# A mixture-of-experts layer on one core: seven of eight row blocks of the experts' weights in two parts, where it was six, and token slots of 26 experts read from a table in DRAM

## The chip, the cores and the metric

The kernel runs on one core of one Trainium2 chip, in one launch. The core has TensorE (PE in the profile, its weight loads PEld), VectorE (DVE), ScalarE (ACT), GpSimd (POOL) and SyncE (SP), which share one on-chip memory and 16 DMA engines. The metric is the device time of one launch in microseconds (us), as the median of several runs.

## The reference

One layer over 1024 tokens of width 1024, all in float32: stick-breaking attention beside a pooling mixer, cross-attention into 256 memory tokens, then a mixture of experts, and a last RMS norm. Only the mixture is touched:

```python
logits = hf @ w_router + b_router             # 1024 tokens, 32 experts
top_val, top_idx = lax.top_k(logits, 4)       # each token goes to 4 experts
gates = jax.nn.softmax(top_val, axis=-1)
# for each expert e, over the tokens routed to it:
gu = xb @ w1[e] + b1[e]                       # w1[e]: 1024 x 2048
gate = jnp.minimum(gu[:, :1024], 7.0)
up = jnp.clip(gu[:, 1024:], -7.0, 7.0)
act = (up + 1.0) * gate * jax.nn.sigmoid(1.702 * gate)
y = (act @ w2[e] + b2[e]) * g[:, None]        # w2[e]: 1024 x 1024, added to the token's row
```

All 32 experts are used, so all of w1 and w2 (32 x 12 MB, 403 MB) is read once.

## The kernel before, in words

The experts run one after the other in the order of the list `ORDER`, from about 835 us of the profiled span to its end; what comes ahead of them (attention, pooling, cross-attention, router) is the same in both kernels. Experts are ranked by their number of tokens, and rank r has room for `CAPS[r]` tokens: 204 down to 130 for ranks 0 to 17 (152.6 on average), and 128 for the other 14. Tokens over an expert's room go through a general loop after the 32 experts.

**The weights.** An expert's weights are 12 pieces of 1 MB: eight of w1, four of w2. A piece holds four row blocks (of 128 of the 1024 inputs) by 512 columns, and two pieces, an even and an odd one, make the eight row blocks of a sum. `load` (L1068) brings a piece in on SP's queue. `split_w` (L1085) then makes two parts of a row block: ScalarE rounds it, scaled by 4096, to the short float32 form that TensorE multiplies in one step (`wh`, L1090), and VectorE computes what is left as float16 (`wl`, L1091). Three row blocks of a piece (`KS = 3`) are treated so, with one instruction on each engine. The fourth stays whole in float32 (`ww`). So two of the eight row blocks of every sum are whole, six are split. `wt`, `wh`, `wl` have six buffers each and `ww` eleven; pieces are split up to `AHEAD = 4` pieces, and loaded up to ten, ahead of the one that TensorE is at.

**The products.** The activations are split as well (`xT` holds the high and low parts side by side, `x16` the float16 copy, `xw` the whole blocks; `act`, `a16`, `aw` for the second product). For the 18 experts with more than 128 tokens (`ffn_wide`, called wide here) the weights are TensorE's stationary operand. `packed` (L1135) computes a group of 128 output columns: for a split row block one float32 matmul of `wh` over 2C columns and one float16 matmul of `wl` over C columns, where C is the room of the expert; for a whole row block one true float32 matmul over C columns, which the profile records as two. An expert has 24 groups of eight row blocks. For the 14 experts of 128 tokens (called split experts here) the activations are stationary and 512 weight columns move: `mm_s` (L1157) issues three matmuls for a split row block (L1163, L1164, L1165) and one (recorded as two) for a whole one (L1166). Such an expert has 6 groups of eight row blocks, and uses its w2 pieces in the order 8, 10, 9, 11.

**The slots.** Each token's place within its expert is known in `posM` before the experts start. For experts 0 and 1 the slots (which token stands in which row, with what gate) are computed ahead. For the other 30, `mark` compares `posM` with a row of numbers on VectorE (`oh`, L1401) and multiplies the resulting ones and zeros by `vals` on TensorE: 8 small matmuls (L1407) for up to 128 rows, 16 above, one expert at a time between the pieces of earlier experts; `settle_set` turns the sums of four experts into `idx` and `sl`. A gather on GpSimd (L1013) brings an expert's tokens into `xg`, TensorE transposes them (L1031), and results are added to the tokens' rows by an indirect DMA (L1118). `extra_table` prepares the general loop while expert 2 runs.

Each engine's instructions run in an order that a scheduler has fixed from the program and a few priorities; an engine takes them strictly in that order.

## Time and profile before

| | |
|---|---|
| median of 3 runs | 2309.15 us (2307.42 to 2311.97) |
| the profiled execution's own time | 2314.93 us |
| its span, first to last instruction | 2313.3 us |
| mean granted TensorE clock in the span | 0.976 of full speed |
| busy: PE, PEld, DVE, ACT, POOL | 94%, 80%, 68%, 59%, 20% of the span |
| DMA | 549.74 MB, mean 238 GB/s |

The rows further down come from one profiled execution. Start times count from its span's start. A granted clock of 1.00 is TensorE's higher level of 2.4 GHz. Matmuls are pipelined, so a row's duration overlaps with the next row: the step between two starts says what an instruction adds.

### The profile page before, as it was taken

Reading aid. Unit: us, or ns where it says so; the run is one execution under the profiler, and the core shown is the slowest. Engines: PE = TensorE matmul, PEld = TensorE weight load, DVE = VectorE, ACT = ScalarE, POOL = GpSimd, SP = SyncE. Lnnn points to the kernel's source line nnn. Section 1 sums busy time; section 2 is a strip of 40 time slices with the busy share of each in tenths; the row PEclk is TensorE's granted clock in tenths of the full one; section 3 lists DMA queues with packets and bytes.
Section 4 is the critical chain, followed back from the end, with each engine's and each line's share of the span. In section 5 each row is a group of like instructions: output and inputs, shape, how many; then the busy total and the mean of one; then the engine's idle time right before and its main releaser. Section 6 shows DMA issues by size and latency. Waiting matters only on the chain. (4 is left out here: it accounts for less than half of the span.)

```text
span 2313.3 us, 41987 instructions
## 1 busy us (share of the span) xinstructions
PE 2180.9 (94%) x15378; PEld 1842.5 (80%) x15378; DVE 1582.5 (68%) x2843; ACT 1357.4 (59%) x2331; POOL 458.3 (20%) x389
## 2 busy tenths in 40 slices
PE   8999998788899969999999999999999999999985
PEld 7989887688899947685899769785898897967972
DVE  5743778865664568767777767777677777776583
ACT  6733556433543147566677667666667676766562
POOL 2101466644242010001111110111011111111002
PEclk9999999899999979999999999999999999999997
DMA  7832123135422279789889998999889989899782
GB/s 246 278 105 60 31 62 92 51 112 171 147 92 74 101 258 370 277 285 351 309 295 312 343 338 287 352 298 357 290 285 333 321 298 333 296 333 341 233 314 75
DMA packets 155621, 549.74 MB, mean 238 GB/s; under 512 B 20453, under 2 KB 24677, under 8 KB 152721
## 3 DMA queue, kind: packets, MB, share of 16 engines
q1 hardware_dynamic: 129024, 478.73, 58.3%
q0 software_dynamic: 16032, 46.21, 8.1%
q10 hardware_dynamic: 10354, 22.06, 2.7%
q8 instruction: 123, 2.02, 0.3%
q14 instruction: 88, 0.72, 0.1%
HBM read 493.16 MB, written 49.57 MB: 235 GB/s over the span
## 5 line engine op out<-in xcount | busy, mean ns | idle before, releaser
L1091 DVE SCALAR_TENSOR_TENSOR wl<-wt,wh 128x1536 f16<-128x1536 f32 x384 | 667.7, 1754 | 187.1 <-ACT wh L1090 162.2
L1090 ACT ACTIVATE wh<-wt 128x1536 fp32r<-128x1536 f32 x384 | 561.9, 1480 | 134.0 <-PE qh L1164 108.8
L1152 PE MATMUL qh<-xT,wh 128*128 128x332 f32 (+17 forms) x1728 | 318.8, 319 | 0.8 <-DVE xT L106 0.5
L1152 PEld LDWEIGHTS qh<-xT,wh 128*128 128x128 f32 x1728 | 251.2, 189 | 2.3 <-DVE xT L106 2.0
L1152 PEld LDWEIGHTS <-wl 128*128 128x128 f16 x2592 | 191.5, 98 | 28.0 <-issue 14.1
L1118 POOL DMA_INDIRECT Adr<-y,idx x50 | 97.6, 1951 | 540.5 <-ACT y L1268 329.8
L1163 PE MATMUL qh<-wh,xT 128*128 128x512 f32 x336 | 201.4, 605 | 1.7 <-ACT wh L1090 1.7
L1242 ACT ACTIVATE gu<-qh,b1P 128x166 f32<-128x166 f32 (+17 forms) x288 | 105.0, 381 | 156.6 <-PE qh L1152 155.8
L1152 PE MATMUL qh<-xw,ww 128*128 128x166 f32 (+17 forms) x1152 | 195.7, 293 | 0.0
L1013 POOL DMA_INDIRECT xg<-Hdr,idx x50 | 63.3, 1266 | 634.4 <-PE qt L1031 590.9
L1152 PE MATMUL qh<-act,wh 128*128 128x332 f32 (+17 forms) x864 | 175.0, 327 | 4.4 <-DVE act L1232 3.3
L1152 PEld LDWEIGHTS qh<-xw,ww 128*128 128x128 f32 x1152 | 169.2, 190 | 0.1
L99 PE MATMUL pd<-uhi,Thi 128*128 128x256 f32 x576 | 165.8, 288 | 2.7 <-ACT pe L756 1.5
L100 PE MATMUL pd<-ulo,Thi 128*128 128x256 f32 x576 | 164.2, 285 | 0.0
L101 PE MATMUL pd<-uhi,Tlo 128*128 128x256 f32 x576 | 163.2, 283 | 0.0
L1152 PE MATMUL qh<-x,wl 128*128 128x166 f16 (+17 forms) x1728 | 146.5, 229 | 4.5 <-ACT x L1061 3.0
L1244 DVE SCALAR_TENSOR_TENSOR gu<-qh,gu 128x166 f32<-128x166 f32 (+17 forms) x288 | 81.7, 311 | 85.4 <-ACT gu L1242 84.2
L1164 PE MATMUL qh<-wh,xT 128*128 128x512 f32 x336 | 135.2, 406 | 0.0
L1152 PEld LDWEIGHTS qh<-act,wh 128*128 128x128 f32 x864 | 128.3, 191 | 6.2 <-DVE act L1232 4.1
L1165 PE MATMUL qh<-wl,x 128*128 128x512 f16 x336 | 131.4, 391 | 0.6 <-DVE wl L1091 0.6
L99 PEld LDWEIGHTS pd<-uhi,Thi 128*128 128x128 f32 x576 | 110.5, 192 | 4.2 <-ACT pe L756 2.0
L1166 PE MATMUL qh<-ww,xw 128*128 128x512 f32 x224 | 113.7, 592 | 0.0
(412 smaller groups left out, 5050.6 us busy)
## 6 DMA issues: line engine op xcount, KB each, us to landing
wt<-w SPq DMA_DIRECT2D x382, 768.0 KB, 6.7
ww<-w SPq DMA_DIRECT2D x382, 256.0 KB, 6.4
w<-wkv SPq DMA_DIRECT2D x8, 1024.0 KB, 7.0
uw<-wout SPq DMA_DIRECT2D x16, 512.0 KB, 4.5
uw<-Mdr SPq DMA_DIRECT2D x16, 512.0 KB, 3.8
w<-win SPq DMA_DIRECT2D x5, 1024.0 KB, 6.0
xt<-x SPq DMA_DIRECT2D x8, 512.0 KB, 3.4
w<-wqT SPq DMA_DIRECT2D x4, 1024.0 KB, 5.7
```

The lines of the kernel that those rows point to most:

```text
L99: nc.tensor.matmul(ps, whi, mhi, start=start, stop=False, **kw)
L100: nc.tensor.matmul(ps, whi, mlo, start=False, stop=False, **kw)
L101: nc.tensor.matmul(ps, wlo, mhi, start=False, stop=stop, **kw)
L1090: last_a[0] = nc.scalar.activation(hi, t, AF.Copy, scale=WS).ins
L1091: nc.vector.scalar_tensor_tensor(lo, t, WS, hi.bitcast(F32), op0=OP.mult, op1=OP.subtract)
L1118: nc.gpsimd.indirect_dma_start(out=Adr, out_offset=bass.IndirectOffsetOnAxis(ap=idx[:m, g, 1:2], axis=0), in_=ys[:m], in_offset=None, comp ...
L1152: nc.tensor.matmul(o, a, b, start=new and n == 0, stop=n == len(jobs) - 1 and KD - 1 in ks, skip_group_check=True)
L1163: nc.tensor.matmul(ps, xhi[:, n], hi[:, k], start=start and k == 0, stop=False, **kw)
L1164: nc.tensor.matmul(ps, xlo[:, n], hi[:, k], start=False, stop=False, **kw)
L1165: nc.tensor.matmul(ps, x16[:, n], lo[:, k], start=False, stop=False, **kw)
L1166: nc.tensor.matmul(ps, xw[:, h], t1, start=False, stop=stop, **kw)
L1242: nc.scalar.activation(t[:, g, f], ph[:, C:2 * C], AF.Identity, scale=1.0 / WS, bias=b1P[:, 8 * g + j, r:r + 1])
```

## The change

`KS` becomes 7 and counts over the whole sum: row blocks 0 to 6 are split, and only block 7, the last of an odd piece, is whole. An even piece comes in one DMA of four blocks (`wt0`), an odd one in a DMA of three (`wt1`) and one of the whole block (`ww`). `split_w` works on four blocks of an even piece and three of an odd one, and each parity has its own three buffers. The split operands `xT`, `x16`, `act`, `a16` hold seven row blocks and `xw`, `aw` one; `ffn_wide` now splits the activation of every block but the last, and `ac` has two buffers instead of three. In `ffn_wide`, 24 row blocks an expert go from whole to split, in a split expert 6.

`mark` remains for experts 2 to 5. For the other 26, VectorE finds for each token its four places in a table (`places`) and the gates (`pick_gates`), while experts 0 and 1 run by the program's order. GpSimd writes 32 times 128 entries of 8 bytes (token and gate) with indirect DMAs into four tables in DRAM (`put`), which ScalarE's queue has filled with zeros before; four DMAs bring them back (`take`) and five VectorE instructions make `idxT` and `slT` of them (`read`) in expert 4 by the program. `extra_table` takes its row of capacities `capt` from a tile filled earlier by 19 memsets, instead of 32 of its own.

```diff
-           'y0'), tags=0, BB=(3,), avs=(0, 1), PS=(2, 3, 2), LAG=1, AB=2, GB=(2,), ORD3=range(0, 8), m3=28, mulL=0, x16=1, a16=1, a16L=1, early=3, ek=(4, 6), wt=6, ww=11, wh=6, wl=6, ahead=10,
-           gu=2, ac=3)
+           'y0'), tags=0, BB=(3,), avs=(0, 1), PS=(2, 3, 2), LAG=1, AB=2, GB=(2,), ORD3=range(0, 8), m3=28, mulL=0, x16=1, a16=1, a16L=1, early=3, ek=(4, 6), wt=(3, 3), ww=6, wh=(3, 3), ahead=10,
+           gu=2, ac=2)
...
-KS = 3
+KS = 7
...
-SLOT_SETS = [[2, 3]] + [list(range(i, i + 4)) for i in range(4, 32, 4)]
+SLOT_SETS = [[2, 3], [4, 5]]
+N2 = sum(c > P for c in CAPS)
+NCOL = NE + N2
+COL = [min(2 * r, r + N2) for r in range(NE)]
...
+    for k in range(4):
+        nc.scalar.dma_start(slot_dr[k].rearrange("(p c) t -> p (c t)", p=P), zr[:, :2 * (NCOL + 1)])
...
-        t = w.tile([P, KS, 512], F32, name="wt")
-        t1 = w.tile([P, 512], F32, name="ww", bufs=PLAN["ww"])
-        (eng or nc.sync).dma_start(t.rearrange("p k n -> p (k n)"), src[:, :KS * 512])
-        ins = (eng or nc.sync).dma_start(t1, src[:, KS * 512:]).ins
+        n = 4 - h
+        t = w.tile([P, n, 512], F32, name=f"wt{h}", bufs=PLAN["wt"][h])
+        t1 = w.tile([P, 512], F32, name="ww", bufs=PLAN["ww"]) if h else None
+        ins = (eng or nc.sync).dma_start(t.rearrange("p k n -> p (k n)"), src[:, :n * 512]).ins
+        if h:
+            ins = (eng or nc.sync).dma_start(t1, src[:, n * 512:]).ins
...
-        hi = w.tile([P, KS, 512], F32R, name="wh", bufs=PLAN["wh"])
-        lo = w.tile([P, KS, 512], F16, name="wl", bufs=PLAN["wl"])
+        hi = w.tile([P, 4 - h, 512], F32R, name=f"wh{h}", bufs=PLAN["wh"][h])
+        lo = w.tile([P, 4 - h, 512], F16, name=f"wl{h}", bufs=PLAN["wh"][h])
...
-        split_k = [k for k in ks if k % 4 < KS]
+        split_k = [k for k in ks if k < KS]
         jobs = []
         for k in split_k:
-            jobs.append((ps[:, :2 * C], parts[k // 4][0][:, k % 4, cs], xT[:, k // 4 * KS + k % 4]))
+            jobs.append((ps[:, :2 * C], parts[k // 4][0][:, k % 4, cs], xT[:, k]))
         for k in ks:
-            if k % 4 == KS:
-                jobs.append((ps[:, :C], parts[k // 4][2][:, cs], xw[:, k // 4]))
-        halves = [(ps[:, :C], parts[k // 4][1][:, k % 4, cs], x16[:, k // 4 * KS + k % 4]) for k in split_k]
+            if k == KS:
+                jobs.append((ps[:, :C], parts[1][2][:, cs], xw))
+        halves = [(ps[:, :C], parts[k // 4][1][:, k % 4, cs], x16[:, k]) for k in split_k]
...
-        for k in range(KS):
-            n = h * KS + k
+        for k in range(4 - h):
+            n = 4 * h + k
             nc.tensor.matmul(ps, xhi[:, n], hi[:, k], start=start and k == 0, stop=False, **kw)
             nc.tensor.matmul(ps, xlo[:, n], hi[:, k], start=False, stop=False, **kw)
             nc.tensor.matmul(ps, x16[:, n], lo[:, k], start=False, stop=False, **kw)
-        nc.tensor.matmul(ps, xw[:, h], t1, start=False, stop=stop, **kw)
+        if h:
+            nc.tensor.matmul(ps, xw, t1, start=False, stop=stop, **kw)
...
-            oh = sb.tile([P, NB, CMAX], BF, name="oh1", bufs=1)[:, :, :C]
+            oh = sb.tile([P, 2, 2, CMAX], F32, name="gu", bufs=PLAN["gu"]).rearrange("p a b c -> p (a b c)")
+            oh = oh.bitcast(BF)[:, :NB * C].rearrange("p (b c) -> p b c", b=NB)
...
+        def places():
+            room = sb.tile([P, 4, NB, NE], F32, name="y1", bufs=1)
+            v, a, b_, _ = (room[:, k] for k in range(4))
+            wide = lambda t: t[:, None, :].to_broadcast([P, NB, NE])
+            nc.vector.tensor_scalar(a, posM, float(P), 1.0 - P * NCOL, op0=OP.is_gt, op1=OP.mult)
+            nc.vector.scalar_tensor_tensor(v, posM, float(NCOL), a, op0=OP.mult, op1=OP.add)
+            nc.vector.tensor_tensor(v, v, wide(colt), op=OP.add)
+            nc.vector.tensor_tensor(a, posM, wide(capt), op=OP.is_le)
+            nc.vector.scalar_tensor_tensor(a, posM, 0.0, a, op0=OP.is_gt, op1=OP.mult)
+            nc.vector.tensor_tensor(v, v, a, op=OP.mult)
+            for b in range(NB):
+                nc.vector.max(picks[:, b], v[:, b])
...
+        def pick_gates(k):
+            v, a = tab["room"][:, 0], tab["room"][:, 2 + k % 2]
+            nc.vector.tensor_tensor(a, v, picks[:, :, k, None].to_broadcast([P, NB, NE]), op=OP.is_equal)
+            nc.vector.tensor_tensor(a, a, GPt, op=OP.mult)
+            nc.vector.tensor_reduce(entry[:, :, k, 1], a, axis=AX.X, op=OP.add)
+        def put(b):
+            for k in range(4):
+                nc.gpsimd.indirect_dma_start(out=slot_dr[k], in_=entry[:, b, k], in_offset=None,
+                                             out_offset=bass.IndirectOffsetOnAxis(ap=place[:, b, k:k + 1], axis=0))
+        def take():
+            for k in range(4):
+                nc.gpsimd.dma_start(table[:, k], slot_dr[k][:P * NCOL].rearrange("(p c) t -> p (c t)", p=P))
+        def read():
+            both = sb.tile([P, 2 * NCOL], F32, name="both", bufs=1)
+            nc.vector.tensor_reduce(both, table.rearrange("p k n -> p n k"), axis=AX.X, op=OP.add)
...
+            for i in range(SLOT_SETS[-1][-1] + 1, NE):
+                cs = slice(COL[ORDER[i]], COL[ORDER[i]] + 1 + (CAPS[ORDER[i]] > P))
+                S[i] = slT[:, cs], idxT[:, cs]
...
-        found, when = {}, {}
-        for n, s_ in enumerate(SLOT_SETS):
-            for m in range(len(s_)):
-                at = [(0, m), (1, m)][n] if n < 2 else (s_[0] - 6 + m, 2)
-                when.setdefault(at, []).append(lambda n=n, m=m: mark(n, m))
-            when.setdefault([(0, 2), (2, 1)][n] if n < 2 else (s_[0] - 3, 2), []).append(lambda n=n: settle_set(n))
+        def places():
+            room = sb.tile([P, 4, NB, NE], F32, name="y1", bufs=1)
+            v, a, b_, _ = (room[:, k] for k in range(4))
+            wide = lambda t: t[:, None, :].to_broadcast([P, NB, NE])
+            nc.vector.tensor_scalar(a, posM, float(P), 1.0 - P * NCOL, op0=OP.is_gt, op1=OP.mult)
+            nc.vector.scalar_tensor_tensor(v, posM, float(NCOL), a, op0=OP.mult, op1=OP.add)
+            nc.vector.tensor_tensor(v, v, wide(colt), op=OP.add)
+            nc.vector.tensor_tensor(a, posM, wide(capt), op=OP.is_le)
+            nc.vector.scalar_tensor_tensor(a, posM, 0.0, a, op0=OP.is_gt, op1=OP.mult)
+            nc.vector.tensor_tensor(v, v, a, op=OP.mult)
+            for b in range(NB):
+                nc.vector.max(picks[:, b], v[:, b])
+            tab["room"] = room
+            p4 = picks[:, :, :4]
+            z = sb.tile([P, NB, 4], F32, name="z4", bufs=1)
+            nc.vector.tensor_scalar(z, p4, 0.0, nowhere[:, 0:1], op0=OP.is_equal, op1=OP.mult)
+            nc.vector.scalar_tensor_tensor(place, p4, -1.0, z, op0=OP.add, op1=OP.add)
+            nc.vector.tensor_copy(entry[:, :, :, 0], tok1[:, :, None].to_broadcast([P, NB, 4]))
+        def pick_gates(k):
+            v, a = tab["room"][:, 0], tab["room"][:, 2 + k % 2]
+            nc.vector.tensor_tensor(a, v, picks[:, :, k, None].to_broadcast([P, NB, NE]), op=OP.is_equal)
+            nc.vector.tensor_tensor(a, a, GPt, op=OP.mult)
+            nc.vector.tensor_reduce(entry[:, :, k, 1], a, axis=AX.X, op=OP.add)
+        def put(b):
+            for k in range(4):
+                nc.gpsimd.indirect_dma_start(out=slot_dr[k], in_=entry[:, b, k], in_offset=None,
+                                             out_offset=bass.IndirectOffsetOnAxis(ap=place[:, b, k:k + 1], axis=0))
+        def take():
+            for k in range(4):
+                nc.gpsimd.dma_start(table[:, k], slot_dr[k][:P * NCOL].rearrange("(p c) t -> p (c t)", p=P))
+        def read():
+            both = sb.tile([P, 2 * NCOL], F32, name="both", bufs=1)
+            nc.vector.tensor_reduce(both, table.rearrange("p k n -> p n k"), axis=AX.X, op=OP.add)
+            t1, gt = both.rearrange("p (c t) -> p t c", t=2)[:, 0], both.rearrange("p (c t) -> p t c", t=2)[:, 1]
+            z = sb.tile([P, NCOL], F32, name="zc", bufs=1)
+            nc.vector.tensor_scalar(idxT[:, :, 0], t1, -1.0, 0.0, op0=OP.add, op1=OP.max)
+            nc.vector.tensor_scalar(z, t1, 0.0, nowhere[:, 1:2], op0=OP.is_equal, op1=OP.mult)
+            nc.vector.scalar_tensor_tensor(idxT[:, :, 1], t1, -1.0, z, op0=OP.add, op1=OP.add)
+            nc.vector.tensor_scalar(slT[:, :, 3], gt, GU, None, op0=OP.mult)
+            for i in range(SLOT_SETS[-1][-1] + 1, NE):
+                cs = slice(COL[ORDER[i]], COL[ORDER[i]] + 1 + (CAPS[ORDER[i]] > P))
+                S[i] = slT[:, cs], idxT[:, cs]
+
+        tab, found = {}, {}
+        when = {(0, 0): [lambda: mark(0, 0)], (0, 1): [lambda: mark(0, 1)], (0, 2): [lambda: settle_set(0)],
+                (0, 3): [places], (2, 0): [lambda: mark(1, 0)], (2, 1): [lambda: mark(1, 1)],
+                (2, 2): [lambda: settle_set(1)], (4, 0): [take], (4, 2): [read]}
+        for k in range(4):
+            when[1, k] = [lambda k=k: pick_gates(k)]
+        for b in range(NB):
+            when.setdefault((2 + b // 4, b % 4), []).append(lambda b=b: put(b))
```

What this does to the order of the engines, at three places. First TensorE, in the middle of a wide expert of 150 tokens: two groups of the first product, before and after (`x` is the float16 copy, `xT` high and low parts, `xw` with `ww` the whole block).

```order
L1152 LDWEIGHTS wl
L1152 MATMUL qh<-x_16590,wl 128x150
L1152 MATMUL qh<-xT,wh 128x300 x6
L1152 MATMUL qh<-xw,ww 128x150 x2
L1152 MATMUL qh<-xT,wh 128x300 x6
L1152 MATMUL qh<-xw,ww 128x150 x2
```

```order
L1162 LDWEIGHTS wl_16507
L1162 MATMUL qh<-x_16461,wl_16507 128x150
L1162 MATMUL qh<-xT,wh_16464 128x300 x4
L1162 MATMUL qh<-xT,wh_16506 128x300 x3
L1162 MATMUL qh<-xw,ww 128x150
L1162 MATMUL qh<-xT,wh_16464 128x300 x4
L1162 MATMUL qh<-xT,wh_16506 128x300 x3
L1162 MATMUL qh<-xw,ww 128x150
```

Each group has seven products of `xT` with `wh` where it had six, and one of `xw` with `ww` where it had two; the float16 products of `wl` (the first rows are the last of them) also become seven a group.

Second VectorE, at the start of the experts, from the first subtraction that makes `xT` of expert 0 to the split of the first pieces of weights; before, then after.

```order
L1304 TENSOR_SCALAR sel<-Pm 96x128
L106 TENSOR_TENSOR xT<-qt,xT 128x3x128
L1091 SCALAR_TENSOR_TENSOR wl<-wt,wh 128x1536
L106 TENSOR_TENSOR xT<-qt,xT 128x3x128
L1091 SCALAR_TENSOR_TENSOR wl<-wt,wh 128x1536 x2
```

```order
L1487 TENSOR_REDUCE entry<-y_9346 128x8
L112 TENSOR_TENSOR xT<-qt,xT 128x4x128
L1487 TENSOR_REDUCE entry<-y_9346 128x8
L1485 TENSOR_TENSOR y_9346<-y_9346,picks 128x256
L112 TENSOR_TENSOR xT<-qt,xT 128x3x128
L1485 TENSOR_TENSOR y_9346<-y_9346,picks 128x256
L1486 TENSOR_TENSOR y_9346<-y_9346,GPt 128x256 x2
L1487 TENSOR_REDUCE entry<-y_9346 128x8
L1101 SCALAR_TENSOR_TENSOR wl_9055<-wt_9052,wh_9054 128x2048
L1487 TENSOR_REDUCE entry<-y_9346 128x8
L1101 SCALAR_TENSOR_TENSOR wl_9063<-wt_9058,wh_9062 128x1536
```

The table's instructions (L1485 to L1487, which the program puts into expert 1) stand in front of the first weights.

Third GpSimd, at the gather for expert 3 (L1013 before, L1021 after), before and after.

```order
L1118 DMA Adr<-y_9314,idx_8820 1152x1024
L982 MEMSET sg 64x1 x9
L1013 DMA xg_10099<-Hdr,idx 128x1024
L982 MEMSET sg 64x1 x23
L1118 DMA Adr<-y_9885,idx_8839 1152x1024
```

```order
L1021 DMA xg_10111<-Hdr,idx 128x1024
L1491 DMA slot_81<-entry,place 6528x2
L1491 DMA slot_82<-entry,place 6528x2
L1491 DMA slot_83<-entry,place 6528x2
L1491 DMA slot_80<-entry,place 6528x2
L1491 DMA slot_81<-entry,place 6528x2
L1491 DMA slot_82<-entry,place 6528x2
L1491 DMA slot_83<-entry,place 6528x2
L1496 DMA table<-slot_80 128x100
L1496 DMA table<-slot_81 128x100
L1496 DMA table<-slot_82 128x100
L1496 DMA table<-slot_83 128x100
```

Of the 32 writes into the tables the last seven, and the four reads, stand behind this gather; the other 25 stand ahead of it, and the 32 memsets are gone.

## Rows read from the trace of the kernel before

**Rows 1.** Engines by window: us, engines' busy time, PEclk, DMA share, GB/s

```profile
1250.00:1500.00 250.00, 248.51 (x1788) 196.51 (x1787) 187.33 (x288) 172.41 (x274) 29.85 (x18) 1.00 0.94 325
...
1729.90:1772.30 42.40, 41.33 (x427) 40.60 (x426) 32.99 (x58) 31.68 (x61) 5.26 (x3) 1.00 0.92 325
1772.30:1812.80 40.50, 40.33 (x180) 22.85 (x178) 32.08 (x42) 28.53 (x38) 6.39 (x4) 1.00 0.98 352
```

**Rows 2.** Waits of PE, 870 to 2290 us: us in total, times, longest

```profile
PE qt L1267 <- DVE yT L1295: 10.2, 3, 7.1
...
PE qh L1152 <- DVE xT L106: 0.5, 3, 0.2
```

**Rows 3.** Page, part 5: busy us, mean ns, idle before and its releaser

```profile
L1091 DVE SCALAR_TENSOR_TENSOR wl<-wt,wh 128x1536 f16<-128x1536 f32 x384 | 667.7, 1754 | 187.1 <-ACT wh L1090 162.2
L1090 ACT ACTIVATE wh<-wt 128x1536 fp32r<-128x1536 f32 x384 | 561.9, 1480 | 134.0 <-PE qh L1164 108.8
```

**Rows 4.** Timeline of PE in a split expert: start us, duration, instruction

```profile
1484.59 0.40 PE L1164 MATMUL qh<-wh,xT 128*128 128x512 f32 x1
...
1485.98 0.40 PE L1164 MATMUL qh<-wh,xT 128*128 128x512 f32 x1
...
1486.45 1.02 PE L1166 MATMUL qh<-ww,xw 128*128 128x512 f32 x2
1487.31 0.38 PE L1323 MATMUL qh<-b1hl,sel 96*128 96x512 bf16 x1
```

**Rows 5.** Timeline of PE in wide experts of 150 and 204

```profile
1515.54 0.96 PE L1152 MATMUL qh<-x,wl 128*128 128x150 f16 x12
...
1517.21 0.67 PE L1152 MATMUL qh<-xw,ww 128*128 128x150 f32 x4
...
1519.06 0.96 PE L1152 MATMUL qh<-x,wl 128*128 128x150 f16 x12
...
2180.79 1.23 PE L1152 MATMUL qh<-x,wl 128*128 128x204 f16 x12
...
2182.99 0.85 PE L1152 MATMUL qh<-xw,ww 128*128 128x204 f32 x4
...
2185.49 1.22 PE L1152 MATMUL qh<-x,wl 128*128 128x204 f16 x12
```

**Rows 6.** Groups by shape on PE, the same experts: busy us, mean ns

```profile
L1152 PE MATMUL qh<-xw,ww 128*128 128x204 f32 x64 | 13.6, 335 | 0.0
...
L1152 PE MATMUL qh<-xw,ww 128*128 128x150 f32 x64 | 10.6, 290 | 0.0
...
L1152 PE MATMUL qh<-x,wl 128*128 128x204 f16 x96 | 10.1, 250 | 1.2 <-DVE gu L1244 1.2
...
L1152 PE MATMUL qh<-x,wl 128*128 128x150 f16 x96 | 8.0, 228 | 0.1
```

**Rows 7.** Groups by line, the marks' matmuls and their weight loads

```profile
L1407 PE MATMUL qs<-vals,oh 128*128 128x6 bf16 (+17 forms) x376 | 15.3, 166 | 0.0
...
L1407 PEld LDWEIGHTS <-oh 128*128 128x128 bf16 (+17 forms) x376 | 13.5, 94 | 4.1 <-issue 1.2 <-DVE ac L1097 1.0
```

**Rows 8.** Timeline of PE at one mark of eight matmuls

```profile
1326.86 0.39 PE L1164 MATMUL qh<-wh,act 128*128 128x512 f32 x1
1327.10 0.35 PE L1407 MATMUL qs<-vals,oh 128*128 128x6 bf16 x8
1327.31 0.38 PE L1165 MATMUL qh<-wl,a 128*128 128x512 f16 x1
```

**Rows 9.** Timeline of DVE, start of the experts; in brackets idle time before

```profile
846.61 0.56 DVE L106 TENSOR_TENSOR xT<-qt,xT 128x384 fp32r<-128x384 f32 x1 [9.03 <-ACT xT L105]
848.54 1.76 DVE L1091 SCALAR_TENSOR_TENSOR wl<-wt,wh 128x1536 f16<-128x1536 f32 x1 [1.37 <-ACT wh L1090]
...
857.71 0.43 DVE L1097 SCALAR_TENSOR_TENSOR ac<-gu,sg 128x256 f32<-128x256 f32 x1 [0.15 <-ACT sg L1096]
```

**Rows 10.** Timeline of DVE at the end of `extra_table`

```profile
960.19 0.18 DVE L996 SCALAR_TENSOR_TENSOR sg<-sg 64x32 f32<-64x32 f32 x1
```

**Rows 11.** Timeline of POOL at expert 3's gather

```profile
930.19 1.01 POOL L1013 DMA_INDIRECT xg<-Hdr,idx  x1 [0.85 <-PE qt L1031]
```

**Rows 12.** DMA issues: count, median us from issue to landing

```profile
Adr<-y,idx POOLq DMA_INDIRECT x50, 10.4
```

**Rows 13.** Page, part 2: GB/s in 40 equal slices of 57.8 us

```profile
GB/s 246 278 105 60 31 62 92 51 112 171 147 92 74 101 258 370 277 285 351 309 295 312 343 338 287 352 298 357 290 285 333 321 298 333 296 333 341 233 314 75
```

More of the change, by code (lines that the diff above doesn't have):

```diff
@@ L96, in block_kernel @@
     tab_dr = dram.tile([NX, 4], F32, name="tab_dr")
+    slot_dr = [dram.tile([P * (NCOL + 1), 2], F32, name=f"slot{k}") for k in range(4)]
     def mm3(ps, whi, wlo, mhi, mlo, start, stop, **kw):
@@ L971, in expert_pools, with extra_table @@
         return w, s, q
-    def extra_table(sb, q):
+    def extra_table(sb, q, capt):
         room = sb.tile([P, 2, CMAX], F32, name="sg", bufs=1).rearrange("p f n -> p (f n)")[:NX]
-        capt, exc, nbk, cum, tmp, sel, tab, _ = (room[:, NE * k:NE * k + NE] for k in range(8))
+        exc, nbk, cum, tmp, sel, tab = (room[:, NE * k:NE * k + NE] for k in range(6))
         tab = tab[:, :4]
@@ L1047, in operand @@
         kw = {} if bufs is None else dict(bufs=bufs)
-        return (sb.tile([P, 2 * KS, n], F32R, name=hl, **kw), sb.tile([P, 2 * KS, C], F16, name=h16, **kw),
-                sb.tile([P, 2, C], F32, name=whole, **kw))
+        return (sb.tile([P, KS, n], F32R, name=hl, **kw), sb.tile([P, KS, C], F16, name=h16, **kw),
+                sb.tile([P, C], F32, name=whole, **kw))
     def parted(src, h, hi, lo, h16, whole, e, n=1):
-        four = lambda t: t.rearrange("p (h k) m -> p h k m", h=2)[:, h:h + n]
-        src = src.rearrange("p (h k) m -> p h k m", h=n)
-        split(four(hi), four(lo), src[:, :, :KS])
-        half(four(h16), four(hi), e)
-        nc.scalar.activation(whole[:, h:h + n], src[:, :, KS], AF.Copy, scale=WS)
+        ks = slice(4 * h, min(4 * h + 4 * n, KS))
+        split(hi[:, ks], lo[:, ks], src[:, :ks.stop - 4 * h])
+        half(h16[:, ks], hi[:, ks], e)
+        if h + n == 2:
+            nc.scalar.activation(whole, src[:, KS - 4 * h], AF.Copy, scale=WS)
     def conv(e, out, src):
@@ L1066, in half, with load @@
         conv(e, out, src.bitcast(F32))
-    def load(w, src, eng=None):
+    def load(w, src, eng=None, h=0):
         ins = []
```

67 lines of the change are left out of this document (42 added, 25 removed).

## The prediction

> **What bounds the kernel now.** I read the windows first, then the waits of TensorE, then the timeline inside an expert. In the window from 1250 to 1500 us, TensorE is busy 248.51 of 250.00 us at a granted clock of 1.00, which is its higher level, while VectorE is busy 187.33 and ScalarE 172.41 [rows 1]. The view of TensorE's waits over 870 to 2290 us has twelve lines; the first holds 10.2 us, the last 0.5 [rows 2], and all twelve add up to about 36 us of 1420. So the experts' stage runs at the speed at which TensorE gets through its list: what shortens the list shortens the kernel, as long as weights stay ready. They are ready with some margin: ScalarE, which rounds a piece, idled 134.0 us before that line, and 108.8 of it ended when TensorE let go of a buffer; VectorE idled 187.1 us before its half of the split, 162.2 of it ended by ScalarE [rows 3]. The splitters wait for TensorE, not it for them.
>
> The tightest company is in a split expert: in 40.50 us VectorE is busy 32.08 us, and the DMA engines show a share of 0.98 at 352 GB/s [rows 1]. That is the first place to look for a new bound.
>
> **TensorE in the split experts.** A split row block is three matmuls. L1164 of one row block starts at 1484.59 and that of the second next at 1485.98 [rows 4], so one costs 1.39 / 2 = 0.695 us. The whole row block starts at 1486.45 and what follows starts at 1487.31: 0.86 us. Converting one saves 0.165 us. There are 14 experts x 6 groups x 1 = 84 of them: **-13.9 us**.
>
> **TensorE in the wide experts.** Three prices are needed, for C = 150 and C = 204. The float16 matmul h comes from a burst of twelve: the burst takes 0.96 us of which one latency is 0.228 [rows 5, 6], so h = (0.96 - 0.228) / 11 = 0.0665; for 204, (1.23 - 0.250) / 11 = 0.089. The whole row block w is two recorded matmuls, and a burst of four takes 0.67 with a latency of 0.290: w = 2 x (0.67 - 0.290) / 3 = 0.253; for 204, 2 x (0.85 - 0.335) / 3 = 0.343. The wh matmul s is what remains of two groups, which hold 12 h, 12 s and 4 w: from 1515.54 to 1519.06 that is 3.52 us, s = (3.52 - 12 x 0.0665 - 4 x 0.253) / 12 = 0.142; for 204, from 2180.79 to 2185.49, 4.70 us and s = 0.188. One conversion saves w - s - h = 0.044 us at 150 and 0.066 at 204. Laid as straight lines through both, w is 1.69 ns a token and s + h is 20 ns + 1.26 ns a token. The 18 experts' mean room is 152.6, where the saving is 0.0453; 18 x 24 = 432 conversions make **-19.6 us**. The line at 131 tokens would give 0.036 (-15.6 us) and the price at 204 throughout 0.066 (-28.5 us): these are the ends that I keep.
>
> **TensorE in the marks.** 336 of the 376 small matmuls go (40 remain for four experts). They were busy 15.3 us in all [rows 7], so 336 / 376 of that is **-13.7 us**. In one mark of eight, the next row starts 0.21 us after the first of them [rows 8], which would be 42 x 0.21 = 8.8 us; if every weight load of 94 ns [rows 7] lay in the open it would be 31.6. The busy time lies near the lower end, since most loads lie beside matmuls.
>
> **What is added at the start.** At the start of the experts VectorE waits 9.03 us before the first subtraction for xT, then 1.37 us for ScalarE's first rounded piece [rows 9]. Most of the table's VectorE work falls into the hole of 9.03 us and is free. What isn't covered: about four instructions of 256 columns that stand ahead of the indices for expert 0's gather, and six between the first xT and the first weights' split. At 0.43 us each (a 128x256 instruction, [rows 9]) that is 1.7 us, and 2.6 less the 1.37 of waiting, 1.2. The first piece, with four blocks to split instead of three, adds ScalarE 1480 / 3 = 493 ns [rows 3]. Together **+3.5 us**; the bounds are 0 (all of it in holes) and 1.7 + 2.6 + 1.1 for both halves of the larger split, 5.4.
>
> **The table.** The gates are complete before the second piece is split, on this trace's scale about 855 us. Each write into a table waits for the one before it in the same table to land, so the 32 go in eight rounds of four. An indirect write's median from issue to landing is 10.4 us [rows 12], though for rows of 4 KB. Six rounds end by 855 + 62 = 917 us, ahead of expert 3's gather at 930.19 [rows 11]. The seven behind it are two rounds, and the read-back one more: 931 + 31 = 962. VectorE's read of the table stands just ahead of the end of `extra_table`, near 960 us [rows 10]: late by 2 us at most by this price, and weights four pieces ahead (`AHEAD = 4`) cover it. Queued behind a waiting read would be the splits of weights, and behind these TensorE. I put it at **+1 us**. If writes took twice as long, VectorE would stand some 40 us and TensorE, after about 13 us of prepared pieces, some 27.
>
> **VectorE and ScalarE.** Of every two pieces the even one is split with one block more: VectorE +1754 / 3 = 585 ns, ScalarE +493 ns [rows 3], for six pieces an expert 3.5 and 3.0 us. In the narrow wide expert VectorE goes from 32.99 to 36.5, ScalarE from 31.68 to 34.6 [rows 1], of an expert that is to take 42.4 - 24 x 0.036 - 0.5 = 41.0 us: shares of 0.89 and 0.84. The comparisons of 28 marks go in return, which I leave as cover. A split that runs 0.585 us longer delays the short instruction behind it, for which TensorE waits at most at two places an expert, at xT and at the activation: 32 x 2 x 0.585 = 37 us at worst, 0 if prepared work always covers it. The few waits of today [rows 2] put it near the lower end: **+5 us**. The SP queue loses 191 of its DMAs of 256 KB, and moves the same bytes; it was never waited for in earnest, so 0.
>
> **The sum.** -13.9 - 19.6 - 13.7 + 3.5 + 1 + 5 = -37.7 us. The profiled execution took 2314.93 us, and becomes 2277.2. It lay 5.8 us over the median of 2309.15, so the median becomes **2271 us**. Its own range reaches down to 2253 with the better end of the wide experts (-8.9), 5 us more from the marks and nothing at the start (-3.5), and up to 2286 with the worse ends of wide experts and marks (+4.0, +4.9) and a third of VectorE's bound (+7) in place of 5, less a little since not all ends meet.
>
> **Rivals.** *VectorE becomes the bound.* For: a share of 0.89 in narrow experts, longer instructions in one strict order. Against: its idle time today ends on ScalarE and TensorE. With the whole 37 us instead of 5: 2303 us; half of it, 2285. Chance 0.12.
>
> *DMA keeps the split experts.* They move 352 GB/s x 40.5 us = 14.3 MB; shortened by 6 x 0.165 = 1.0 us each, they would need 361 GB/s. Against: one slice of the page shows 370 GB/s over 57.8 us [rows 13]. For: a share of 0.98. If they stay at 40.5 us, 13.9 us are lost: 2285 us. Chance 0.08. The Trainium skill speaks against the change here: "DMA: Bandwidth & Descriptors", section Specifications, gives about 358 GB/s as the limit of memory for one core. By that rule such an expert could not go under 14.3 MB / 358 GB/s = 39.8 us, 0.3 us more than planned, 14 times: an estimate of 4 us more. The slice at 370 GB/s does not agree with it (both counts are of all bytes moved), so nothing is added for it.
>
> *Slower: buffers by parity.* Six buffers that any piece could take become three for even and three for odd pieces. In a split expert, with its order 8, 10, 9, 11, piece 10 must wait for piece 4's buffer, and the next expert's piece 3 for piece 9's, one piece later than now. If the splits no longer keep a piece's lead, TensorE stands for one piece, 40.5 / 12 = 3.4 us, at two places in 14 experts: +95 us, so 2366. It decides only if the lead falls to nothing, which the idle time of the splitters speaks against. At 0.4 of this price the gain is gone. Chance 0.05.
>
> *The change does not do what it says.* If a wide conversion saves nothing, because what TensorE is charged is the time of weight loads rather than of columns, the 19.6 us stay: 2291. The measured groups at two widths speak against it. Chance 0.05.
>
> **How the numbers follow.** My forecast has 0.70. The range of 8 in 10 goes from 2253, where the good ends meet, to 2291, which takes in the DMA rival, the wide conversions at nothing and the better half of VectorE's. A measurement of this kernel tells about 0.2% (4.6 us) from no change. Slower by more than that: the parity rival and mishaps with the table, 0.05. Within: the worst of VectorE's and combinations, 0.04. Faster: 0.91.
>
> **What would show it.** In the profile after, a step between whole and split groups as computed: two groups at C = 150 in 3.52 - 2 x 0.044 = 3.43 us; a split expert in 39.5 us near 360 GB/s; 40 small matmuls; TensorE's waits in the stage under 45 us. The forecast is wrong if TensorE waits for `wl` or `act` by more than 30 us, if VectorE stands at the read of the table for more than 15 us, or if split experts stay at 40 us and over.

## The result: 3% slower, and the profile after

| | before | changed |
|---|---|---|
| median | 2310.56 us (2307.42 to 2315.71, 4 runs) | 2380.15 us (2377.29 to 2390.66, 4 runs) |
| ratio to before, 95% interval | | 1.0301 [1.0281, 1.0321] |
| span of the profiled execution | 2313.3 us | 2375.6 us |
| TensorE's last instruction | 2290.0 us | 2344.7 us |
| TensorE's waits, 870 us to 60 us ahead of that | 24.7 us, 10 of over 1 us | 94.5 us, 44 of over 1 us |
| time at TensorE's lower clock (1.2 GHz), 870 us to 40 us ahead of it | 13.7 us in 2 stretches | 85.3 us in 18 stretches |

The forecast was 2271 us, with a range of 2253 to 2291. The last three rows are sums over TensorE's instructions and the clock records of each trace, and are given for the experiments too.

The list of TensorE did shrink as forecast. Two groups of a wide expert of 150 tokens after the change (timeline of TensorE: start, duration):

```profile
1555.15 1.10 PE L1162 MATMUL qh<-x,wl 128*128 128x150 f16 x14
...
1558.57 1.10 PE L1162 MATMUL qh<-x,wl 128*128 128x150 f16 x14
```

They take 3.42 us; before they took 3.52 [rows 5], and 3.43 was forecast. But TensorE no longer works without pause. The windows after (columns as in [rows 1]) are a split expert, a wide one of 131 tokens and the long stretch, and then the same long stretch of the kernel before:

```profile
1810.80:1854.60 43.80, 39.67 (x176) 22.71 (x174) 33.91 (x32) 31.88 (x37) 8.22 (x4) 1.00 0.85 320
1766.30:1810.80 44.50, 41.32 (x411) 40.25 (x409) 35.00 (x57) 33.90 (x59) 6.47 (x3) 0.96 0.89 311
870.00:2290.00 1420.00, 1325.36 (x9438) 1077.75 (x9437) 1054.66 (x1519) 988.86 (x1471) 211.96 (x125) 0.97 0.85 302
```

```profile
870.00:2290.00 1420.00, 1382.68 (x9914) 1119.14 (x9912) 1031.68 (x1687) 946.90 (x1580) 163.55 (x133) 0.99 0.89 309
```

The split expert takes 43.8 us instead of 40.5, with DMA at a share of 0.85 instead of 0.98; the wide one 44.5 instead of 42.4. TensorE's waits over 870 to 2290 us, after (total, times, longest):

```profile
PE qh L1174 <- DVE act L112: 23.7, 16, 3.0
PE qh L1162 <- DVE gu L1250: 21.8, 13, 1.9
PE qt L1039 <- DVE xT L112: 14.8, 16, 1.5
PE qh L1162 <- ACT a L1069: 11.2, 9, 3.0
PE qh L1173 <- ACT act L111: 6.7, 5, 1.5
...
```

Before, the largest line was three waits for `yT` [rows 2], and the line that is now the first, VectorE's `act` in a split expert, was the ninth:

```profile
PE qh L1164 <- DVE act L106: 1.4, 2, 1.2
```

What TensorE waits for now are short results of VectorE and ScalarE, in every expert: the halves of the activations, and the freeing of its sums. The two split instructions after (columns as in [rows 3]):

```profile
L1101 DVE SCALAR_TENSOR_TENSOR wl<-wt,wh 128x1536 f16<-128x1536 f32 (+1 forms) x384 | 768.8, 2022 | 229.3 <-ACT wh L1100 225.5 <-PE qh L1162 1.6
L1100 ACT ACTIVATE wh<-wt 128x1536 fp32r<-128x1536 f32 (+1 forms) x384 | 642.1, 1694 | 129.9 <-PE qh L1174 101.8 <-PE qh L1162 13.1 <-DMA wt<-w 10.8
```

How a wait comes about is seen in the timeline of a split expert after the change (start, duration, idle time before in brackets):

```profile
1523.20 1.91 ACT L1100 ACTIVATE wh<-wt 128x2048 fp32r<-128x2048 f32 x1 [1.90 <-PE qh L1174]
...
1525.15 2.29 DVE L1101 SCALAR_TENSOR_TENSOR wl<-wt,wh 128x2048 f16<-128x2048 f32 x1 [1.97 <-ACT wh L1100]
...
1527.36 0.68 DVE L112 TENSOR_TENSOR xT<-qt,xT 128x512 fp32r<-128x512 f32 x1
...
1528.10 0.66 PE L1039 MATMUL qt<-ident,xg 128*128 128x128 f32 x4 [1.48 <-DVE xT L112]
1528.15 2.29 DVE L1101 SCALAR_TENSOR_TENSOR wl<-wt,wh 128x2048 f16<-128x2048 f32 x1
...
1530.36 0.55 DVE L112 TENSOR_TENSOR act<-qt,act 128x384 fp32r<-128x384 f32 x1
...
1530.96 0.51 PE L1174 MATMUL qh<-wh,act 128*128 128x512 f32 x1 [1.68 <-DVE act L112]
```

ScalarE stands until TensorE lets go of a buffer, VectorE stands until ScalarE has rounded, then the 2.29 us split runs, and the 0.6 us instructions that TensorE is waiting for stand behind both.

The clock goes with it. After two waits of TensorE near 1570 us (first fence), the granted clock of the next 3.5 us is at the lower level, 1.2 GHz (second fence, windows):

```profile
1570.10 0.29 PE L1162 MATMUL qh<-a,wl 128*128 128x150 f16 x2 [0.94 <-ACT a L1069]
1572.19 0.57 PE L1162 MATMUL qh<-a,wl 128*128 128x150 f16 x6 [1.80 <-DVE gu L1250]
```

```profile
1567.50:1573.30 5.80, 3.06 (x30) 2.63 (x28) 5.70 (x9) 5.80 (x12) 0.00 (x0) 1.00 0.89 332
1573.30:1576.80 3.50, 3.50 (x18) 3.17 (x18) 0.32 (x2) 0.51 (x3) 0.00 (x0) 0.51 0.90 330
```

The balance of the experts' stage goes over the whole stretch from 870 us to TensorE's last instruction. It takes in a wait of 7.1 us in the kernel before [rows 2], which ended near 2233 us and so lies in the last 60 us, outside the 24.7 of the table. The waits grow from 36.4 to 100.4 us, +64. Of the additional 72 us at the lower level, half is counted as lost, +36. The stage's end moved by 54.7, so the list must have become some 45 us shorter; 47 were forecast (33.5 for the converted row blocks, 13.7 for the marks). The end of the kernel adds 7.6 us more: a chain of DMAs that GpSimd issues for the last rows starts after a norm on VectorE, and the span ends 56 to 58 us after that start in both, but the start lies 25 us ahead of TensorE's last instruction instead of 35. Its first issue, before and then after:

```profile
2255.36 2.73 POOL L1187 DMA_INDIRECT xg<-Adr,idx  x1 [13.05 <-DVE rs_a L131]
```

```profile
2319.78 2.23 POOL L1198 DMA_INDIRECT xg<-Adr,idxT  x1 [20.80 <-DVE rs_y L125]
```

### The profile page after: what moved, and what is told of

Read it like the earlier page. It is cut to its first block, busy times and chain, and to the rows that moved or that the text cites. A ratio compares the mean times of both kernels' runs of the same rounds, so it can differ in the third digit from the quotient of the medians.

```text
span 2375.6 us, 40547 instructions
## 1 busy us (share of the span) xinstructions
PE 2173.6 (91%) x15120; PEld 1832.0 (77%) x15120; DVE 1661.6 (70%) x2804; ACT 1428.8 (60%) x2266; POOL 531.5 (22%) x411
## 5 line engine op out<-in xcount | busy, mean ns | idle before, releaser
L1101 DVE SCALAR_TENSOR_TENSOR wl<-wt,wh 128x1536 f16<-128x1536 f32 (+1 forms) x384 | 768.8, 2022 | 229.3 <-ACT wh L1100 225.5
L1100 ACT ACTIVATE wh<-wt 128x1536 fp32r<-128x1536 f32 (+1 forms) x384 | 642.1, 1694 | 129.9 <-PE qh L1174 101.8
L1162 PEld LDWEIGHTS qh<-xT,wh 128*128 128x128 f32 x2016 | 291.9, 189 | 1.6 <-DVE xT L112 1.5
L1173 PE MATMUL qh<-wh,xT 128*128 128x512 f32 x392 | 224.9, 579 | 2.7 <-ACT wh L1100 2.7
L1128 POOL DMA_INDIRECT Adr<-y,idxT x42 | 89.0, 2118 | 594.8 <-ACT y L1274 393.7
L1162 PE MATMUL qh<-act,wh 128*128 128x332 f32 (+17 forms) x1008 | 215.3, 343 | 5.5 <-DVE act L1240 5.5
L1174 PE MATMUL qh<-wh,xT 128*128 128x512 f32 x392 | 162.5, 416 | 0.0
L1021 POOL DMA_INDIRECT xg<-Hdr,idxT x42 | 64.4, 1534 | 438.0 <-PE qt L1039 435.2
L1162 PE MATMUL qh<-a,wl 128*128 128x166 f16 (+17 forms) x1008 | 111.2, 241 | 33.0 <-DVE gu L1250 21.8
L1162 PE MATMUL qh<-xw,ww 128*128 128x166 f32 (+17 forms) x576 | 120.5, 293 | 0.0
L1173 PE MATMUL qh<-wh,act 128*128 128x512 f32 x196 | 109.8, 584 | 8.2 <-ACT act L111 7.9
```

The lines of the kernel that those rows point to most:

```text
L1100: last_a[0] = nc.scalar.activation(hi, t, AF.Copy, scale=WS).ins
L1101: nc.vector.scalar_tensor_tensor(lo, t, WS, hi.bitcast(F32), op0=OP.mult, op1=OP.subtract)
L1128: nc.gpsimd.indirect_dma_start(out=Adr, out_offset=bass.IndirectOffsetOnAxis(ap=idx[:m, g, 1:2], axis=0), in_=ys[:m], in_offset=None, comp ...
L1162: nc.tensor.matmul(o, a, b, start=new and n == 0, stop=n == len(jobs) - 1 and KD - 1 in ks, skip_group_check=True)
L1173: nc.tensor.matmul(ps, xhi[:, n], hi[:, k], start=start and k == 0, stop=False, **kw)
L1174: nc.tensor.matmul(ps, xlo[:, n], hi[:, k], start=False, stop=False, **kw)
```

## The experiments

The columns are: median, ratio to before with its 95% interval, then from the profiled execution TensorE's last instruction, its waits, its time at the lower clock (as in the table above), and the time from its last instruction to the end of the span. Before, in the sessions of the experiments: 2314.0 to 2315.8 us (2310.6 beside the changed kernel), and 2290.0, 24.7, 13.7, 23.3. The scheduler lays out every engine's order anew for each kernel, so a run can differ from its neighbour by more than its edit.

| run | us | ratio | PE end | waits | low clock | tail |
|---|---|---|---|---|---|---|
| changed | 2380.2 | 1.030 [1.028, 1.032] | 2344.7 | 94.5 | 85.3 | 30.9 |
| e1 weights only | 2454.4 | 1.059 [1.056, 1.063] | 2403.3 | 126.4 | 153.6 | 48.1 |
| e2 table only | 2311.4 | 0.998 [0.996, 0.999] | 2285.5 | 29.2 | 20.5 | 26.2 |
| e4 splits in two | 2361.2 | 1.019 [1.016, 1.021] | 2313.0 | 71.9 | 95.6 | 46.0 |
| e7 splits in four | 2372.4 | 1.025 [1.023, 1.027] | 2340.1 | 87.3 | 99.0 | 32.3 |
| e5 AHEAD = 3 | 2382.5 | 1.029 [1.026, 1.031] | 2350.2 | 98.8 | 95.6 | 29.1 |
| e6 old, parity pools | 2322.9 | 1.005 [1.003, 1.006] | 2299.6 | 36.1 | 17.1 | 20.9 |
| e9 smaller load buffers | 2413.1 | 1.043 [1.041, 1.046] | 2366.3 | 108.4 | 119.5 | 45.2 |
| e8 the same, shared pool | 2419.1 | 1.046 [1.040, 1.051] | 2394.8 | 118.2 | 126.3 | 29.6 |
| e10 work as before | 2340.6 | 1.010 [1.008, 1.012] | 2303.6 | 58.9 | 71.7 | 35.5 |
| e11 VectorE as before | 2364.6 | 1.022 [1.020, 1.024] | 2321.7 | 78.5 | 68.3 | 36.2 |
| e12 ScalarE as before | 2374.3 | 1.025 [1.023, 1.027] | 2345.4 | 82.6 | 92.2 | 33.8 |
| e13 residue on GpSimd | 2423.0 | 1.046 [1.044, 1.049] | 2377.2 | 116.4 | 119.5 | 44.9 |
| x4 old, new PE list | 2350.1 | 1.015 [1.013, 1.018] | 2292.2 | 67.6 | 34.1 | 45.8 |
| x5 old, ac = 2 | 2315.5 | 1.000 [0.999, 1.002] | 2292.3 | 24.6 | 17.1 | 23.2 |
| x6 e10, shared, ac = 3 | 2322.0 | 1.003 [1.002, 1.005] | 2281.4 | 52.1 | 37.5 | 35.5 |
| x9 x4, less splitting | 2257.6 | 0.977 [0.974, 0.979] | 2223.6 | 11.6 | 3.4 | 32.5 |
| x10 e2, splits in two | 2331.0 | 1.008 [1.006, 1.010] | 2301.5 | 48.9 | 30.7 | 25.3 |
| x11 x4, wide only | 2356.7 | 1.019 [1.016, 1.022] | 2314.9 | 61.5 | 44.4 | 39.1 |

**Which half.** e1 takes the table away, e2 is the table in the kernel before.

```diff
# e1, on the changed kernel (marks for 30 experts, no table)
-SLOT_SETS = [[2, 3], [4, 5]]
+SLOT_SETS = [[2, 3]] + [list(range(i, i + 4)) for i in range(4, 32, 4)]
```

> The changed kernel with the old slots: marks for 30 experts again, no table in DRAM; the weights in seven split row blocks and the buffers stay as changed. Theory W (the weights' half of the change makes TensorE wait: about 60 us more waits in the experts' stage and some 40 us of lower clock behind them): it stays slow, 2380 to 2400 us, since 336 small matmuls (about 14 us) come back and a few us of the table go. Theory T (the table is what makes it slow): 2275 to 2300 us, faster than before.

> The kernel before with the table in DRAM alone: six row blocks split as before, six shared buffers, marks for four experts only. Theory W: 14 us of small matmuls go and about 5 us come at the start, so 2297 to 2305 us, with TensorE's waits in the stage near 40 us. Theory T: 2340 us and over.

Theory W holds: the table alone is 0.2% faster than before, the weights' half alone far slower. e1 came out 54 us above its range: its marks' ones and zeros lie in the buffers of `gu`, as in the changed kernel, and its largest wait is for `act` in wide experts (46.6 us), so it is no clean measure of the half's size. The gain of e2 is 5 us where the prediction's terms for marks, start and table gave 9; its 2311 us lie 6 above the range expected.

**Long instructions or buffers.** In the changed kernel:

```diff
# e4 (e7: one row block each)
-        last_a[0] = nc.scalar.activation(hi, t, AF.Copy, scale=WS).ins
-        nc.vector.scalar_tensor_tensor(lo, t, WS, hi.bitcast(F32), ...)
+        for ks in (slice(0, 2), slice(2, 4 - h)):
+            last_a[0] = nc.scalar.activation(hi[:, ks], t[:, ks], AF.Copy, scale=WS).ins
+            nc.vector.scalar_tensor_tensor(lo[:, ks], t[:, ks], WS, hi[:, ks].bitcast(F32), ...)
# e5
-AHEAD = 4
+AHEAD = 3
# e9
-wt=(3, 3), ww=6
+wt=(2, 3), ww=4
# e8: e9 and
-        hi = w.tile([P, 4 - h, 512], F32R, name=f"wh{h}", bufs=PLAN["wh"][h])
+        hi = w.tile([P, 4, 512], F32R, name="wh", bufs=6)[:, :4 - h]      # lo alike
# e6, on the kernel before
-        hi = w.tile([P, KS, 512], F32R, name="wh", bufs=PLAN["wh"])
+        hi = w.tile([P, KS, 512], F32R, name=f"wh{h}", bufs=3)            # lo, wt alike
```

> The changed kernel, but every split of a piece is made by two instructions on each engine (two row blocks, then two or one) instead of one of four or three. Theory L (the longer split instructions of 1.9 us on ScalarE and 2.3 us on VectorE hold up the short ones behind them): the longest wait for a short instruction halves, waits fall by 25 to 40 us with the lower clock behind them, 2310 to 2345 us. Theory B (a split stands first in ScalarE's and VectorE's order and waits until TensorE lets a buffer go, the activations' work stands behind it): the waiting time for a buffer is the same, so 2370 to 2390 us.

> The changed kernel with every split made by one instruction for each row block (four or three on each engine instead of one). Theory L: the waits that were left with two instructions (72 us in the stage) fall again, below 55 us, TensorE ends the stage 15 us or more before it does with two (2313 us), and the time is 2320 to 2350 us. Theory B, or an order that happened to be better with two: no further gain, 2355 to 2385 us.

> The changed kernel with weights split up to three pieces ahead instead of four (AHEAD = 3); buffers as changed, three for each parity. Theory B: with one piece less in hand a buffer has been let go by the time its split is due, ScalarE and VectorE hardly stand, TensorE's waits fall towards 40 us and the time to 2270 to 2310 us. Theory L: the instructions are as long as in the changed kernel and one piece less is in hand, so 2375 us or slower.

> The kernel before with its six shared buffers of wt, wh and wl made three for even and three for odd pieces; three row blocks of a piece split, as before. Theory B (buffers by parity come free a piece later and make the splits stand): TensorE's waits rise from 25 to 60 us and more, 2340 us and over. Theory L (the longer instructions): nothing changes, 2305 to 2320 us.

> The changed kernel with wt = (2, 3) and ww = 4 alone, as the thing to compare the shared buffers with. Both theories: 2375 to 2395 us, since loads were never waited for; over 2400 us would say that fewer loaded pieces in hand cost time by themselves.

> The changed kernel with six buffers of wh and six of wl that any piece can take (each large enough for four row blocks); to make room, two buffers instead of three for an even piece as loaded and four instead of six for the whole block. Theory B: TensorE's waits in the stage fall below 50 us, 30 us or more faster than the run beside it with the same smaller load buffers. Theory L: the same as that run within 10 us.

Two instructions bring 19 us, and the stage ends 32 us sooner, of which the tail takes 15 back; 2361 us lies between the ranges of the two theories. Four bring less than two, which theory L did not expect; 2372 us is in the range given for theory B or for the order. e5 says nothing: in the experts ScalarE's and VectorE's instructions came out in the same order as in the changed kernel. By parity the old kernel loses 9 us (2323, between the two ranges), and the shared pool gains nothing over e9: by these runs theory B is a small part. x6, further down, finds 19 us. e9 missed its range: with fewer load buffers ScalarE waits for the weights themselves, which it hardly did in the changed kernel (10.8 us). Its first line of ScalarE's waits:

```profile
ACT wh L1100 <- DMA wt<-w: 108.0, 56, 4.8
```

**The added work.** In e10 an even piece is split as far as before:

```diff
-        last_a[0] = nc.scalar.activation(hi, t, AF.Copy, scale=WS).ins
+        last_a[0] = nc.scalar.activation(hi, t[:, :3], AF.Copy, scale=WS).ins     # VectorE alike
-            jobs.append((ps[:, :2 * C], parts[k // 4][0][:, k % 4, cs], xT[:, k]))
+            jobs.append((ps[:, :2 * C], parts[k // 4][0][:, min(k % 4, 2), cs], xT[:, k]))
# e13
+            nc.gpsimd.tensor_scalar(t[:, 3], t[:, 3], WS, None, op0=OP.mult)
+            nc.gpsimd.tensor_tensor(lo[:, 3], t[:, 3], hi[:, 3].bitcast(F32), op=OP.subtract)
```

> The changed kernel, but ScalarE and VectorE make only three row blocks of an even piece, as long as their instructions were before; TensorE multiplies the third one twice in place of the fourth (its list, the DMAs and the buffers' number are as changed; the fourth row block's weights are left out of the result). Theory Q (the added 3.0 and 3.5 us an expert on ScalarE and VectorE are what makes TensorE wait): waits in the stage fall to 25 to 45 us and the time to 2265 to 2285 us, what the prediction's sum gave. Theory R (something else of the change: buffers, three to two of ac, the order, a shorter TensorE list that leaves the others no time): 2330 us and over.

> As the one before, but ScalarE rounds all four row blocks and only VectorE's instruction is as short as it was (the residue of the third row block is used twice; that of the fourth is left out of the result). Theory V (VectorE's length is the larger part): 2280 to 2310 us. Theory A (ScalarE's is, since VectorE stands waiting for ScalarE): 2335 to 2375 us.

> The counterpart: ScalarE rounds three row blocks of an even piece, VectorE's instruction is as long as in the changed kernel (the fourth residue is made with a wrong row block of rounded weights, and TensorE multiplies the third rounded block twice). Theory V: 2335 to 2375 us. Theory A: 2280 to 2310 us.

> The whole computation of the changed kernel, with the residue of the fourth row block of an even piece made by two instructions on GpSimd (a scaling in place and a subtraction) instead of VectorE. GpSimd has some 30 of 40 us of an expert to spare; six times two instructions of 512 columns should be 15 to 25 us. Theory V: near the run with VectorE as before, 2285 to 2320 us, if GpSimd's result comes in time. Theory A: 2350 us and over.

The added work costs 40 us (2380 to 2341). Taking out VectorE's part alone brings 16, ScalarE's alone 6, so neither theory V nor theory A holds: each had one of the two runs at 2280 to 2310 us, and they took 2365 and 2374. And the added work is not the whole: with no more splitting than before, the kernel is still 25 us slower than before, as theory R has it. GpSimd makes it worse, 43 us over the changed kernel: its two instructions took 2.55 and 1.92 us, 27 us in an expert where 15 to 25 were expected, and VectorE's instruction of three row blocks took 1.96 us instead of 1.755. How much of the 43 us comes from either is not shown.

**TensorE's list alone.** x4 edits nothing but the products, in the kernel before; x9 also splits one row block less of every piece on ScalarE and VectorE.

```diff
# x4, on the kernel before, in packed (mm_s alike)
-        split_k = [k for k in ks if k % 4 < KS]
+        split_k = [k for k in ks if k != 7]
+        m3 = lambda k: min(k % 4, KS - 1)
-            if k % 4 == KS:
+            if k == 7:
# x9, on x4
-        last_a[0] = nc.scalar.activation(hi, t, AF.Copy, scale=WS).ins
+        last_a[0] = nc.scalar.activation(hi[:, :2], t[:, :2], AF.Copy, scale=WS).ins   # VectorE alike
# x5, on the kernel before                     # x6, on e10
-gu=2, ac=3                                    -name=f"wh{h}", bufs=PLAN["wh"][h]
+gu=2, ac=2                                    +name="wh", bufs=6      # wl alike, and ac=3
```

> The kernel before with nothing changed but TensorE's list in the experts: seven split row blocks and one whole in every sum. The fourth row block of an even piece, which would need its own split, is replaced by the third one used twice (it is left out of the result); ScalarE's and VectorE's work, the buffers, the DMAs and the marks stay as before. Theory P (a shorter list shortens the time by what it saves, 33.5 us, as the prediction's sum has it): 2273 to 2285 us. Theory S (the slack was used up: a shorter list leaves ScalarE and VectorE no time, and waits and a lower clock take the gain back): 2300 us and over.

> The kernel before with two buffers of ac instead of three. If the buffers of ac are part of the cause: 10 to 30 us slower than before. If not: the same within 5 us.

> The run with three row blocks split of every piece (e10: the fourth row block of an even piece left out of the result), with six buffers of wh and wl for any piece instead of three by parity, and three of ac. If buffers are what is left of the loss: 2270 to 2300 us. If TensorE's shorter list or the order is: within 12 us of e10's 2341.

> TensorE's list of x4 (seven split and one whole row block in every sum, the rest as in the kernel before), and ScalarE and VectorE split only two row blocks of a piece, about 1.0 and 1.2 us instead of 1.5 and 1.75; TensorE uses the second one for those that are missing (left out of the result). Theory S (no room: the splits' time in ScalarE's and VectorE's order holds up what TensorE waits for): waits in the stage fall from 68 to under 35 us, 2270 to 2295 us. Theory O (the order of the new list, whatever the room): over 2315 us.

> The whole computation: the kernel before with the table in DRAM (as in e2) and every split made by two instructions on each engine, of two row blocks and one. If shorter instructions let TensorE's short results through sooner in the old split too: 2290 to 2305 us, the best so far. If the order matters more: between 2305 and 2330 us.

> As x4, with the shorter list in the 18 wide experts only (the split experts' list stays; the fourth row block of an even piece is left out of the result in the wide experts). If the loss of x4 sits in the wide experts: within 15 us of x4's 2350. If it sits in the split experts, whose ScalarE and VectorE are the busiest: 2285 to 2305 us.

In x4 a shorter list does not move the end of TensorE's work (2292.2 against 2290.0). From 870 us to that end, its waits are 70.8 us against 36.4 and the lower clock costs 10 us more, so its list must be some 42 us shorter (33.5 by the prediction's prices; the same balance gives 42 for x9), and all of it is taken back. The chain at the end of the kernel is 22.5 us longer. The profiled execution was the fastest of the four, 2339.6 us; what makes the median 10 us slower still, no trace shows. Its largest line of waits over 870 to 2290 us, and the first line of x9's:

```profile
PE qt L1269 <- DVE yT L1297: 33.6, 13, 3.4
```

```profile
PE qt L1270 <- DVE yT L1298: 6.3, 6, 1.4
```

One of these waits, in the expert of 150 tokens, in the timeline of x4:

```profile
1554.21 1.05 ACT L1296 ACTIVATE yT<-qh 128x150 f32<-128x150 f32 x5
...
1554.41 3.42 DVE L1091 SCALAR_TENSOR_TENSOR wl<-wt,wh 128x1536 f16<-128x1536 f32 x2 [2.79 <-ACT wh L1090]
1557.75 0.75 DVE L1297 TENSOR_TENSOR yT<-qh,yT 128x150 f32<-128x150 f32 x3
1558.20 0.45 PE L1269 MATMUL qt<-ident,yT 128*128 128x128 f32 x1 [3.39 <-DVE yT L1297]
```

and the same place in the kernel before:

```profile
1546.30 1.38 ACT L1294 ACTIVATE yT<-qh 128x150 f32<-128x150 f32 x5
1546.61 0.54 DVE L1295 TENSOR_TENSOR yT<-qh,yT 128x150 f32<-128x150 f32 x2 [2.11 <-ACT yT L1294]
...
1547.18 0.38 PE L1267 MATMUL qt<-ident,yT 128*128 128x128 f32 x2
```

In x4 VectorE stands 2.79 us for ScalarE's rounded weights, then makes two splits of 1.7 us; ScalarE's five `yT` were ready by 1555.3, and TensorE stands 3.39 us. In the kernel before VectorE stood for `yT` instead, and TensorE not at all.

So x4 differs from the kernel before in more than its edit. At this place the kernel before has two halves of `yT` ahead of the split in VectorE's order, and x4 has two splits ahead of all of them. In x4 that is so in nine of the 18 wide experts, and TensorE waits 29.9 us for `yT` in these nine, 3.8 us in the other nine; in the kernel before it is so in three. Whether the shorter list would have gained with the order of the kernel before was not tested.

x9 has the shorter list with splits of 1.2 us instead of 1.75 on VectorE: it is 57 us faster than before, TensorE waits 11.6 us, and the clock stays up. Its order is new again, but at like places it shows what the length of a split does: both splits stand ahead of the halves in six wide experts, and cost TensorE 0.7 to 1.4 us in each, where each of x4's nine cost 3.2 to 3.4. x11 puts the loss of x4 into the wide experts: it has the same nine places with the same 29.9 us.

x5 clears `ac` in the kernel before: there ScalarE's and VectorE's instructions in the experts are in the same order; x6 shows that pools and `ac` together are 19 us of e10, which e6 and x5 by themselves do not add up to. Along the kernels that have the table, the loss of the weights' half thus falls in three: 40 us for the added work (changed to e10), 19 for pools and `ac` (e10 to x6), and 11 for what is left between x6 and e2 (2322.0 and 2311.4).

x10, the table with the splits in two, which had helped in the changed kernel, is slower than e2 by 20 us. Of the kernels that compute the whole reference, e2 is the fastest, and it is 0.2% faster than before.

## Why the prediction was wrong

**What bounds the kernel now: this step failed.** The prediction took TensorE's 248.51 of 250 us as the sign that its list alone sets the time ("what shortens the list shortens the kernel, as long as weights stay ready"), and the other engines' idle time as cover. In the changed kernel the list did become some 45 us shorter, no line of TensorE's waits above names the weights, and yet the stage became 54.7 us longer: TensorE stood for short results that were queued behind splits in VectorE's and ScalarE's fixed orders. VectorE's 187.1 us of idle time ahead of the split [rows 3] were counted as room. In the place shown of x4 such idle time is time in which VectorE *stood* for rounded weights, with `yT` ready behind the split. x9 shows what shorter splits are worth: the same list as x4, with instructions that are 30% shorter (1.22 us for 1.755 on VectorE, 1.05 for 1.48 on ScalarE), gives more than the sum of the prediction. That the kernel before stood at a balance, with no room at all for a shorter list, is not shown, since x4's order was worse too.

**The prices of TensorE's instructions** held: 3.42 us for two groups at 150 tokens where 3.43 was forecast, and some 45 us for the whole list where 47 was.

**VectorE and ScalarE, +5 us, at worst 37.** In place of the 5 us the trace shows 100: 64 of waits and 36 of lower clock. The mechanism was named, as the first rival, and its price was wrong in kind: it counted the 0.585 us by which an instruction grows, at two places an expert. What stands ahead of a short instruction is a whole split, sometimes two, and the standing ahead of it: 1.5 and 1.7 us in the split expert shown, 3.4 in x4. With the shares of 0.79 and 0.76 in the narrow expert, 0.89 and 0.84 were never reached, since TensorE's waits stretched the expert. The lower clock had no term at all, nor had the end of the kernel, +7.6 us. Two of the signs that the prediction had set against itself came out: TensorE waits 35.9 us for `act` (23.7, 6.7 and 5.5 in the lines above), and the split expert shown takes 43.8 us.

**DMA** did not decide: its share in a split expert fell from 0.98 to 0.85. **Buffers by parity** were overpriced in kind: e6 gives 9 us, not 95, with more waits on `act` (8.9 us on VectorE's, 1.4 before) and none on a missing piece; with the new list the pools and `ac` were worth 19 (x6). **The table** came in time, as forecast: VectorE's read starts at 960.55 us with no wait ahead of it (timeline of VectorE).

```profile
960.55 0.88 DVE L1501 TENSOR_REDUCE both<-table 128x100 f32<-128x400 f32 x1
```

**What stays open.** No run has the shorter list with the order of the kernel before. Similar kernels differ by 10 to 20 us in ways that no single edit explains: four instructions a split being worse than two, x10 worse than e2, the tail between 21 and 48 us. How much of the 40 us of added work, and of the last 25 us of e10, lies in the order, and how much in room that the shorter list takes away, was not separated.
